# One branch at the end for all the seldom tiles of a sparse expert layer

## The chip, the cores and the metric

The kernel runs on one core of a Trainium2 chip. The metric is the device time of one launch in microseconds (us). Before the change it was 1567.93 us, the median of three runs (1567.35 to 1574.56).

## What is computed

The reference is one decoder layer for 2048 tokens of width 1024: a mixer (sliding-window attention, a gated linear recurrence and a forgetting attention, all from one input projection), then a hierarchical mixture of experts, then a final RMSNorm. The change lies in the mixture of experts. Each token picks one of 4 groups by its group logits, and in that group the best two of 4 experts:

```python
group_p, group_idx = lax.top_k(group_prob, 1)
top_p, top_local = lax.top_k(expert_prob, TOP_K)
weights = group_p * top_p / jnp.sum(top_p, axis=-1, keepdims=True)
for e in range(N_EXPERTS):
    hidden = jax.nn.silu(h @ w_gate[e]) * (h @ w_up[e])
    y = y + combine[..., e:e + 1] * (hidden @ w_down[e])
```

How many tokens go to an expert is known only once the router has run. The kernel computes an expert for its own tokens alone.

## The kernel before

**Lists.** The router (`router`, `place`) handles the 16 blocks of 128 tokens, a few at a time. It marks for each token its two experts and its group, counts marks per list with matmuls against a triangle and against ones, and scatters the token's number into 20 lists in HBM (`list_d`): one for each of the 16 experts (`NE`), and one for each of the 4 groups (`NL` = 20 in all). The list of the last group leaves out the tokens of the last expert. After the last block a matmul of ones with `cumM` gives the 20 lengths, and VectorE copies them as integers into `ci` (line 1072). At expert 0, line 1367 loads every length from `ci` into a register of each of the five engines, 20 loads on each.

**Experts.** `body(e)` computes two tiles of 128 tokens of expert e without a condition: a gather of token rows (`gather`), transposes (`x_T`), the gate and up products (`gates`), the down products (`down`), and a scatter with add into the residual stream in HBM (`add`). `chain(e, 2)` then covers a third tile and beyond: a branch on "length over 256" (line 1482) whose body computes a tile and holds the branch for the next one, 14 levels deep. A weight fetch for a later expert goes on SP's queue meanwhile.

**Final norm.** The tokens of a group can be normed and written when the group's four experts have been added. `fetch_done` and `fin_get` gather a finished group's tiles from the stream, `fin_rs` and `fin_scale` norm them (line 1539 is the scaling), and `fin_put` writes them to the output (line 1546). Six tiles (768 tokens) of each of the groups 0 to 2 are done so without a condition, two at a time within the bodies of later experts. `fin_chain(g, 6)` covers what a group has beyond 768 tokens: a branch (line 1554) around one tile and the next branch, 10 levels. For group 0 it stands after expert 6, for group 1 after expert 10.

**End.** `last_body` handles expert 15 and finishes that expert's tokens directly (`finish`, lines 1462 to 1469), with the two static tiles of the last group beside them. After the last write three blocks follow one another: `chain(15, 2)`, `fin_chain(2, 6)` and `fin_chain(3, 2)`.

**Order.** The program is written in order, and a planner with a simulated timeline places each instruction on its engine's queue. A conditional block is placed as one unit: nothing from outside goes between its instructions. `after(...)` and `behind(...)` add order edges by hand. Each engine runs the branch for itself when its own queue comes to it. An engine that jumps over a block afterwards brings up to date the semaphores that the block would have counted. In the records these are EVENT_SEMAPHORE and, for the DMAs that GpSimd (POOL) would have issued, INC_SWDGE_SEM; they stand under the line of the branch. Line 1624 is the end of the program: DRAIN, and semaphores between the engines.

## Time and profile before

| what | value |
|---|---|
| median of 3 runs | 1567.93 us |
| the profiled execution's own time | 1562.93 us |
| its span (first to last instruction) | 1561.1 us |
| mean granted clock of TensorE | 0.951 |
| instructions | 22860 |

The profiled execution was 5.00 us shorter than the median of the three runs, and 1.83 us of its time lie outside its span. PE is TensorE's matmul, PEld its weight load, DVE is VectorE, ACT is ScalarE, POOL is GpSimd and SP is SyncE; a name with a q after it (POOLq, DVEq) is that engine's sequencer, which runs branches, semaphores and register loads. Times in a row are us from the start of the span, unless marked ns.

### The profile page before, as it was taken

What the parts mean: (1) busy time and instruction counts of PE and PEld (TensorE: products, weight loads), DVE (VectorE), ACT (ScalarE), POOL (GpSimd) and SP (SyncE); (2) the same over time, 40 slices, a digit from 0 to 9 for tenths busy, and PEclk for the clock granted to TensorE, in tenths of its full rate; (3) what the DMA queues carried; (4) which work ended last, traced back from release to release, by engine and by line L of the source; (5) the groups of instructions that cost most, each with busy time, mean ns of one, the idle gap of its engine ahead of it and who ended that gap; (6) DMA issues with size and microseconds to landing.
All of it is one profiled execution on the core that took longest, in us unless ns stands there. A gap on an engine that the chain in (4) does not pass through costs nothing. (4 is left out here: it accounts for less than half of the span.)

```text
span 1561.1 us, 22860 instructions
## 1 busy us (share of the span) xinstructions
PE 1408.7 (90%) x6896; PEld 1131.8 (72%) x6896; DVE 1081.9 (69%) x2838; ACT 759.3 (49%) x1505; POOL 583.3 (37%) x662
## 2 busy tenths in 40 slices
PE   4799999989999899998899999995999998998981
PEld 4677789778898577776678877784777776776760
DVE  5767656745655998988856797785775665566664
ACT  5365234655655688987744232322553533343341
POOL 4210014102224554637704443433344434434452
PEclk9799999999999899999989999996999999999995
DMA  9527983156668856325164343325777868677954
GB/s 323 161 81 246 329 295 115 53 153 181 173 184 238 218 142 196 115 62 156 48 207 138 112 174 122 121 78 157 232 216 204 244 181 254 154 223 230 275 144 159
DMA packets 177087, 276.91 MB, mean 177 GB/s; under 512 B 31161, under 2 KB 120265, under 8 KB 176864
## 3 DMA queue, kind: packets, MB, share of 16 engines
q1 hardware_dynamic: 151184, 212.33, 43.4%
q0 software_dynamic: 25680, 62.09, 14.8%
q8 instruction: 81, 1.33, 0.4%
q14 instruction: 142, 1.16, 0.2%
HBM read 209.90 MB, written 89.03 MB: 191 GB/s over the span
## 5 line engine op out<-in xcount | busy, mean ns | idle before, releaser
L53 PE MATMUL sc<-R,R 128*128 128x512 f32 (+1 forms) x1352 | 324.7, 393 | 9.1 <-ACT R L131 5.4
L53 PEld LDWEIGHTS sc<-R,R 128*128 128x128 f32 x1352 | 249.4, 191 | 67.4 <-issue 7.8
L53 PE MATMUL sc<-R,yh 128*128 128x512 f32 x512 | 170.8, 412 | 10.0 <-DVE x L973 6.7
L855 POOL DMA_INDIRECT xg<-h_d,LT x55 | 63.4, 1153 | 171.3 <-PE sc L53 38.2
L53 PEld LDWEIGHTS sc<-R,yh 128*128 128x128 f32 x512 | 95.1, 193 | 32.6 <-DVE x L973 10.3
L132 DVE TENSOR_TENSOR ptlo<-tp,pthi 128x512 fp32r<-128x512 f32 (+3 forms) x162 | 98.1, 624 | 20.1 <-ACT pthi L131 19.6
L53 PE MATMUL sc<-R,hh 128*128 128x512 f32 x328 | 102.1, 413 | 3.8 <-DVE R L1462 3.1
L53 PE MATMUL sc<-R,fq 128*128 128x512 f32 (+3 forms) x320 | 96.8, 402 | 8.1 <-DVE fmx L287 4.5
L53 PE MATMUL sc<-R,yl 128*128 128x512 f32 x256 | 103.2, 404 | 0.0
L131 ACT ACTIVATE pthi<-tp 128x512 fp32r<-128x512 f32 (+3 forms) x162 | 85.0, 547 | 33.6 <-PE tp L306 15.1
L973 DVE SCALAR_TENSOR_TENSOR x<-sc,r,x 128x512 f32<-128x512 f32 x96 | 71.4, 746 | 41.4 <-PE sc L53 34.4
L53 PE MATMUL pv<-w,xh 128*128 128x512 f32 x256 | 84.3, 411 | 5.4 <-ACT xh L131 2.8
L53 PE MATMUL pv<-R,xh 128*128 128x512 f32 x256 | 85.5, 417 | 2.1 <-PEq L1482 0.9
L295 POOL TENSOR_SCALAR row<-row,frs 128x640 f32<-128x640 f32 (+11 forms) x48 | 71.7, 1495 | 38.5 <-DVE frs L294 32.1
L306 PEld LDWEIGHTS tp<-ident,row 128*128 128x128 f32 x504 | 62.8, 141 | 29.0 <-issue 14.0
L132 DVE TENSOR_TENSOR R<-R,R 128x512 fp32r<-128x512 f32 (+1 forms) x128 | 81.9, 698 | 0.3 <-ACT R L131 0.3
L306 PE MATMUL tp<-ident,row 128*128 128x128 f32 x504 | 78.5, 274 | 0.9 <-POOL row L295 0.9
L1128 POOL DMA_INDIRECT list_d<-vals,spots x48 | 50.6, 1054 | 70.9 <-DVE spots L1105 29.0
L131 ACT ACTIVATE R<-R 128x512 fp32r<-128x512 f32 (+1 forms) x130 | 73.3, 642 | 6.0 <-DMA R<-in_w_down 3.7
L53 PEld LDWEIGHTS sc<-R,hh 128*128 128x128 f32 x328 | 61.4, 196 | 17.0 <-DVE R L1462 3.8
L131 ACT ACTIVATE xh<-tp 128x512 fp32r<-128x512 f32 x82 | 45.4, 596 | 56.4 <-PE tp L1264 49.2
L293 ACT ACTIVATE row<-row,fmx 128x640 f32<-128x640 f32 (+11 forms) x48 | 68.0, 1416 | 8.5 <-DVE fmx L287 8.3
(414 smaller groups left out, 3439.2 us busy)
## 6 DMA issues: line engine op xcount, KB each, us to landing
x<-in_x SPq DMA_DIRECT2D x32, 512.0 KB
x<-in_w_mod SPq DMA_DIRECT2D x32, 512.0 KB
R<-in_w_gate SPq DMA_DIRECT2D x128, 128.0 KB
R<-in_w_up SPq DMA_DIRECT2D x128, 128.0 KB
R<-in_w_down SPq DMA_DIRECT2D x32, 512.0 KB
wraw<-in_w_inT SPq DMA_DIRECT2D x24, 512.0 KB
R<-kc_d SPq DMA_DIRECT2D x80, 128.0 KB
wm<-in_w_mod SPq DMA_DIRECT2D x32, 256.0 KB
```

The lines of the kernel that those rows point to most:

```text
L53: return PE.matmul(o, l, r, start=first, stop=last)
L131: return (ACT.activation(hi, src, AF.Copy), (lo_eng or V).tensor_tensor(lo, src, f32(hi), op=ALU.subtract))
L132: (lo_eng or V).tensor_tensor(lo, src, f32(hi), op=ALU.subtract))
L293: ACT.activation(row[:, 0:n], row[:, 0:n], AF.Exp, bias=prev, scale=-1.0, accum_out=rs)
L295: G.tensor_scalar(row[:, 0:n], row[:, 0:n], rs, 1.0, op0=ALU.mult, op1=ALU.mult)
L306: PE.transpose(p[:, r * 128:(r + 1) * 128], rows[r][:, j * 128:(j + 1) * 128], ident)
L855: return G.indirect_dma_start(out=dst, out_offset=None, in_=h2_d[:, :], in_offset=bass.IndirectOffsetOnAxis(ap=idx, axis=0), **(dict(bound ...
L973: V.scalar_tensor_tensor(x1[:, sl], p, r3s[t][:, g:g + 1], x1[:, sl], op0=ALU.mult, op1=ALU.add)
L1128: d = G.indirect_dma_start(out=list_d[:, :], out_offset=bass.IndirectOffsetOnAxis(ap=di[:, i, s:s + 1], axis=0), in_=vals[:, t0 + i, s, :] ...
```

## The change

The three branches at the end become one, on a new register, and the two branches in the middle go. The router computes the new number: `most` holds for each list how many tokens are covered without a condition (256 for expert 15 and group 3, 768 for groups 0 to 2, more than there can be for the other experts), a comparison with the lengths gives 20 zeros or ones, and their sum goes to `ci` as a 21st entry. The first 15 lengths and that entry are loaded into registers at expert 0, 16 loads for 20; the other five lengths are loaded inside the new block. Inside it stand the old three blocks and those of groups 0 and 1, whose lists are loaded again there.

```diff
+        most, seldom = cn.tile([1, NL], F32, name="most"), cn.tile([1, 1], F32, name="seldom")
+        V.memset(most, float(FAR))
+        V.memset(most[:, NE:NL - 1], 768.0)
+        for l in (NE - 1, NL - 1):
+            V.memset(most[:, l:l + 1], 256.0)
...
-                V.tensor_copy(ci, pc[0:1, 0:NL])
+                V.tensor_copy(ci[:, 0:NL], pc[0:1, 0:NL])
+                over = wk.tile([1, NL], F32, name="over", bufs=1)
+                V.tensor_tensor(over, pc[0:1, 0:NL], most, op=ALU.is_gt)
+                V.tensor_reduce(seldom, over, axis=AX.X, op=ALU.add)
+                V.tensor_copy(ci[:, NL:NL + 1], seldom)
...
-        ci = pers.tile([1, NL], I32, name="ci")
+        ci = pers.tile([1, NL + 1], I32, name="ci")
...
+        def length(l):
+            nreg[l] = nc.values_load_multi_w_load_instructions(ci[0:1, l:l + 1], ...)[1][0]
...
-                    for l in range(NL):
-                        nreg.append(nc.values_load_multi_w_load_instructions(ci[0:1, l:l + 1], ...)[1][0])
+                    for l in list(range(NE - 1)) + [NL]:
+                        length(l)
...
             with after([last]):
+                seldom_tiles(e)
+
+        def seldom_tiles(e):
+
+            with tc.If(nreg[NL] > 0):
+                for l in range(NE - 1, NL):
+                    length(l)
                 chain(e, 2)
+                fin_chain(NG - 1, 2, xg[1])
                 fin_chain(NG - 2, 6, xg[1])
-                fin_chain(NG - 1, 2, X5[nx[0] % 4])
+                for g in range(NG - 2):
+                    list_load(LG[g % 2], NE + g)
+                    fin_chain(g, 6, xg[1])
...
             if e < NE - 1:
                 chain(e, 2)
-            if e % 4 == 2 and 4 < e < NE - 2:
-                fin_chain(e // 4 - 1, 6, xg[1])
```

## Rows read from the trace of the kernel before

**Rows 1.** The page: busy us of each engine, share of the span, instructions.
```profile
PE 1408.7 (90%) x6896; PEld 1131.8 (72%) x6896; DVE 1081.9 (69%) x2838; ACT 759.3 (49%) x1505; POOL 583.3 (37%) x662
```

**Rows 2.** Stretches: start:end, us, busy us of PE, PEld, DVE, ACT, POOL, clock, DMA.
```profile
1500.00:1561.00 61.00, 25.65 (x95) 18.53 (x93) 32.68 (x98) 12.48 (x27) 22.65 (x20) 0.67 0.49 149
```

**Rows 3.** Order of time, POOL, last row: start, us, instruction, idle before it.
```profile
1546.15 0.97 POOL L1546 DMA_INDIRECT out_dram<-xg,LG  x1 [0.69 <-DVE xg L1539]
```

**Rows 4.** Line 1482 after 1540: ns min/median/max, first and last start.
```profile
L1482 POOLq EVENT_SEMAPHORE  x4: 17/43/43, 1546.4 to 1550.9; - x4
...
L1482 DVEq EVENT_SEMAPHORE  x1: 21/21/21, 1547.6 to 1547.6; - x1
L1482 POOLq INC_SWDGE_SEM  x1: 1088/1088/1088, 1551.0 to 1551.0; - x1
```

**Rows 5.** Line 1554 after 1540, the two later blocks of the end.
```profile
L1554 DVEq EVENT_SEMAPHORE  x2: 21/21/21, 1551.3 to 1554.8; - x2
L1554 POOLq INC_SWDGE_SEM  x2: 1073/1076/1079, 1552.8 to 1555.3; - x2
```

**Rows 6.** Line 1624, the end of the program.
```profile
L1624 POOLq DRAIN  x3: 50/114/3872, 1556.4 to 1560.9; - x3
```

**Rows 7.** Line 1554 on POOL over the whole span: branches at four places.
```profile
L1554 POOLq COMPARE_BRANCH  x4: 45/45/45, 1269.5 to 1553.9; - x4
```

**Rows 8.** Line 1554 on POOL from 1265 to 1280, the block of group 0.
```profile
L1554 POOLq EVENT_SEMAPHORE  x4: 17/43/43, 1269.9 to 1274.1; - x4
```

**Rows 9.** Order of time, POOL, around that block.
```profile
1269.74 1.80 POOL L1546 DMA_INDIRECT out_dram<-X,LG  x1 [14.13 <-DVE X L1539]
1275.95 1.33 POOL L1546 DMA_INDIRECT out_dram<-X,LG  x1 [4.41 <-DVE yo L1290]
```

**Rows 10.** Stretches of experts 6, 7, 9 and 11 (a branch of TensorE to the next).
```profile
1233.00:1249.40 16.40, 15.59 (x76) 12.32 (x77) 12.79 (x26) 11.80 (x24) 11.22 (x8) 1.00 0.87 219
1263.70:1282.70 19.00, 16.73 (x79) 12.74 (x80) 16.29 (x36) 11.91 (x24) 7.63 (x5) 1.00 0.48 149
1345.90:1362.10 16.20, 15.76 (x77) 12.75 (x78) 12.74 (x25) 9.83 (x20) 12.90 (x9) 1.00 0.82 217
1395.90:1414.70 18.80, 17.02 (x79) 12.93 (x80) 16.40 (x36) 11.92 (x24) 8.21 (x5) 1.00 0.46 144
```

**Rows 11.** TensorE's waits, 1200 to 1480: total, times, longest us.
```profile
PE tp L1272 <- DVEq L1482: 10.6, 6, 3.6
PE sc L53 <- DVE hl L132: 2.9, 2, 1.7
PE tp L1264 <- DMA xg<-h_d,LT: 2.8, 3, 1.5
```

**Rows 12.** Line 1482 on DVE from 1284 to 1294, expert 7's branch.
```profile
L1482 DVEq COMPARE_BRANCH  x1: 56/56/56, 1286.4 to 1286.4; - x1
L1482 DVEq EVENT_SEMAPHORE  x1: 21/21/21, 1292.0 to 1292.0; - x1
```

**Rows 13.** The same from 1476 to 1482, expert 13's branch.
```profile
L1482 DVEq COMPARE_BRANCH  x1: 56/56/56, 1477.4 to 1477.4; - x1
L1482 DVEq EVENT_SEMAPHORE  x1: 21/21/21, 1478.3 to 1478.3; - x1
```

**Rows 14.** Line 1367, the register loads.
```profile
L1367 SPq TENSOR_LOAD <-ci x20: 15/266/473, 1065.0 to 1089.2; - x20
...
L1367 ACTq TENSOR_LOAD <-ci x20: 275/280/478, 1082.8 to 1089.7; - x20
```

**Rows 15.** Order of time, DVE, at the end of the router.
```profile
1064.82 0.17 DVE L1072 CAST ci<-pv 1x20 int32<-1x20 f32 x1 [0.71 <-PE pv L53]
1066.12 0.16 DVE L1080 COPY rk<-pv 128x1 f32<-128x1 f32 x1 [1.13 <-PE pv L53]
```

**Rows 16.** Order of time, TensorE, from the router's end into expert 0.
```profile
1065.04 0.62 PE L53 MATMUL pv<-Ms,before 128*128 128x20 f32 x2 [0.26 <-DVE ci L1072]
...
1098.07 1.06 PE L1264 MATMUL tp<-ident,xg 128*128 128x128 f32 x8 [2.92 <-DMA xg<-h_d,LT]
```

## The prediction before the run

> **What bounds the kernel now.** The page's first part says TensorE: its matmuls are busy for 90% of the span, VectorE for 69% [rows 1]. That is an average, so the second view read is the table of stretches. In the last one TensorE works 25.65 us of 61.00 [rows 2]: the end of the program is bound by something else. The third view is the order of time at that end, and with it the records that the sequencers leave under the branch lines. POOL's last real work is the output write issued at 1546.15, 0.97 us long [rows 3], yet the span runs to 1561.1. So 14.0 us pass after it, and that is where the three branches stand. The fourth view is the list of TensorE's waits among the experts: 10.6 us in six waits end when VectorE gets past a branch of line 1482, 2.9 us with a VectorE result, 2.8 us with a gather [rows 11].

> **Whether the branches are taken.** Line 1554 has four sites in the program, and POOL shows four compares there [rows 7]; a taken one would show the next level's compare too. So no group has more than its static tiles. The count of the new register is a sum over the same comparisons, so it is zero and the new block is jumped over.

> **Part 1: three branches at the end become one.** A compare itself costs 45 ns [rows 7]. What costs is what follows it. On POOL the first block (line 1482) ends like this: its last EVENT_SEMAPHORE is at 1550.9, then INC_SWDGE_SEM from 1551.0 for 1.088 us, so to 1552.1 [rows 4]. The two blocks of line 1554 repeat branch, semaphores and INC_SWDGE_SEM; the second of these starts at 1555.3 and takes 1.07 us, to 1556.4 [rows 5]. POOL's DRAIN follows at 1556.4 and takes 3.872 us [rows 6], and everybody waits for it. The later two rounds are therefore 1556.4 - 1552.1 = 4.3 us, on the path. With one block POOL goes from 1552.1 straight to the DRAIN.

> The first round is not cheaper after the change. Its last semaphore at 1550.9 comes 3.8 us after the last write was issued (1546.15 + 0.97 = 1547.1), and I read it as a wait for that write to land; in the middle of the program the same four semaphores end at 1274.1, 2.6 us after a write issued by 1271.5 [rows 8, 9]. That wait also covers what the other engines need. VectorE gets past its first branch at 1547.6 and its later ones cost it until 1551.3 and 1554.8 [rows 4, 5], 3.7 and 3.5 us each; one jump instead of three leaves it ready before 1550.9. If POOL's own jump over the bigger block takes as long as VectorE's 3.7 us, it ends at 1549.6, still under the landing. Bounds: nothing gained, if the DRAIN ends when it does for another reason; up to 6.9 us, if two thirds of its 3.872 us (2.6 us) is the work of the two increments that go. I take 4.3, since the DRAIN starts in the row right where the last increment ends.

> [...]

> **Part 2: the two branches in the middle go.** At expert 6 POOL issues the first of two output writes at 1269.74, then meets the branch, whose semaphores run to 1274.1, so that the second write comes at 1275.95 instead of about 1271.9 [rows 8, 9]. POOL's queue behind it (gathers, adds) is 4 us late; expert 10 has the same, once. What does TensorE feel? Experts 7 and 11, behind those blocks, take 19.0 and 18.8 us from branch to branch, experts 6 and 9 take 16.4 and 16.2 [rows 10]. Three more matmuls at 0.21 us (15.59 by 76) are 0.6 of it. So 2.1 and 1.9 us are in excess. But not all of it is the branch: the two waits for a VectorE result, 2.9 us with the longest 1.7 [rows 11], stand behind the scaling of a finished pair of tiles, which stays (VectorE is busy for 16.3 us there, against 12.8 [rows 10]). That leaves 4.0 - 2.9 = 1.1 us. Of the three waits for a gather, 2.8 us with 1.5 the longest, I take one to come from POOL's late queue and count 1.1 us for it. Part 2 gives 2.2 us. Bounds: 0, if TensorE finds its data as late as before, and 4.0 + 1.1 = 5.1.

> **Part 3: four register loads fewer on each engine.** SP takes 24 us in all for its loads, with other DMAs between, ScalarE 20 loads from 1082.8 to 1090.0, 0.36 us each [rows 14]; four fewer are 1.4 us on ScalarE. Beside them TensorE waits 2.92 us, but for a gather that ends at 1098.07 [rows 16], which needs the lists and not ScalarE. So ScalarE's gain is covered. SP issues the list loads between its register loads; a pass there is three instructions, (1089.2 - 1065.0) / 19 = 1.3 us with all that lies between, and the loads' own 0.27 us bounds it from below. If all four went ahead of the lists, TensorE's 2.92 us would shrink by at most that. If instead the loads wait for the new entry of the same tile, they start some 0.5 us later. Bounds: 2.9 gained, 0.6 lost. I take 0.2 gained: what the planner puts ahead of the lists is set by when SP finds its weight buffers free.

> **Part 4: three small VectorE operations in the last step of the router.** The nearest rows are the copy to `ci`, 0.17 us, and the next copy, 0.16 us, which waits 1.13 us for TensorE [rows 15]. Reduce and cast fit in that wait. The comparison doesn't quite: it reads the bank that TensorE's next matmul waits for (0.26 us for the copy [rows 16]), so that matmul starts 0.1 to 0.2 us later, in a chain where nothing else runs. At worst all three stand there, 0.6 us; at best none, 0. I take 0.2 lost. The four memsets stand at the router's start, where TensorE has work of its own, and are single rows; cover gone, they cost a few tenths. The loads of the other five lengths, and the list loads on SP, lie inside the block and are jumped.

> **The sum.** -4.3 - 2.2 - 0.2 + 0.2 = -6.5 us. The profiled execution took 1562.93 us (span 1561.1 and 1.83 around it), so its like after the change takes 1556.4. The median of the runs stood 5.00 us above it, and I keep that: 1567.93 - 6.5 = 1561.4, or 0.41% less. With the terms' likely play its own range is 1558.5 to 1565. 0.5%, about what a measurement of this kernel can tell from no change, is 7.8 us: faster begins below 1560.1, slower above 1575.8.

> **Rivals.**
> - *The middle gives more.* Experts 7 and 11 fall to the length of 6 and 9 (5.1 us with the gather), and the end gives 4.3 to 6.9: 1555.9 to 1558.5, say 1557. For it: DMA share in these stretches is 0.48 and 0.46 against 0.87 and 0.82, POOL issues 5 against 8 and 9 [rows 10], so more than TensorE is held up. Against it: VectorE's scaling stays.
> - *Slower: VectorE's fetch behind the expert branches falls worse.* At expert 13 it goes on 0.9 us after the compare [rows 13], at expert 7 only after 5.6 us, of which TensorE idles 3.6 [rows 11, 12]. Which of the two a branch meets should depend on where its target lies in VectorE's stream, and taking two blocks out of that stream moves every target from expert 7 to 14. Each branch that turns from quick to slow costs up to 3.6 us. Two use up the gain (1561.4 + 7.2 = 1568.6, from where it is slower than before), three give 1572, four 1575.8. Against it: the slow ones can turn quick as well, and with 10.6 us in six waits, 3.6 the longest, several are slow already.
> - *The end is held by something else* (the DRAIN ends when it ended, or a branch really costs no more than its compare), and the middle gives nothing: about 1567.8, two compares of 45 ns less. Against it are the DRAIN's start and VectorE's 3.5 us behind a jump [rows 5, 6].
> - *The block is taken*: then it costs five loads and at least one further round of tile, gather and write. Rows 7 exclude it for these inputs.

> **How the numbers follow.** The forecast gets 0.48, the better middle 0.25, the worse fetch 0.17, the held end 0.08, the taken block 0.02. Faster by over 0.5%: the better middle and a third of the forecast's own range, 0.40. Slower by over 0.5%: the worse fetch with four branches or more and half of the taken block, 0.06. Within: 0.54. The range reaches from 1554 (both upper bounds of the parts 1 and 2, with no more) to 1571 (between two and three branches worse).

> **What would show it.** Part 1: one INC_SWDGE_SEM after the last output write, the DRAIN about 1 us after that write's landing, and 9.7 us instead of 14.0 from the last write to the end. If the DRAIN grows by what the rounds lose, part 1 is wrong. Part 2: POOL's two output writes of expert 6 next to one another, and stretches of experts 7 and 11 nearer 18 us. Part 3: 16 loads in each queue, TensorE's wait before expert 0's second transposes still near 2.9 us. Part 4: the wait behind the copy to `ci` near 0.4 us. The waits on VectorE's branch tell the slower rival: 10.6 us now; above 17 it has come true.

## The result, and the profile after

The changed kernel took 1551.72 us (median of 7 runs, 1550.02 to 1557.07), the kernel before beside it 1567.35 us (7 runs). Its time is 0.9929 of that of before, 95% interval [0.9900, 0.9958]: 11.1 us less (6.6 to 15.7 by the interval). A second set (experiment 11) gave 0.9949 [0.9926, 0.9971], 8.0 us less (4.5 to 11.6). On the 1567.93 us of the prediction these are 1556.8 and 1559.9 us; the forecast was 1561.4. Single runs of one kernel lie up to 1.5% apart, so what follows goes by ratios of many runs and by stretches of the profile. The profiled execution took 1554.04 us (span 1552.2), for 1562.93 before.

**The end.** The changed kernel's last row of POOL in order of time, then its line of the new branch after 1538 (ns min/median/max, first and last start), then the end of the program. They answer to [rows 3 to 6].

```profile
1542.08 0.96 POOL L1569 DMA_INDIRECT out_dram<-xg,LG  x1 [0.69 <-DVE xg L1562]
```
```profile
L1461 POOLq EVENT_SEMAPHORE  x5: 17/43/43, 1545.0 to 1545.9; - x5
...
L1461 DVEq EVENT_SEMAPHORE  x2: 21/21/21, 1543.4 to 1543.5; - x2
L1461 DVEq COMPARE_BRANCH  x1: 56/56/56, 1540.5 to 1540.5; - x1
L1461 POOLq COMPARE_BRANCH  x1: 53/53/53, 1541.8 to 1541.8; - x1
L1461 POOLq INC_SWDGE_SEM  x1: 1110/1110/1110, 1546.0 to 1546.0; - x1
```
```profile
L1645 POOLq DRAIN  x3: 46/109/3872, 1547.1 to 1551.6; - x3
```

One round stands where three stood. The last write ends at 1542.08 + 0.96 = 1543.0, the last semaphore comes at 1545.9, the increment ends at 1547.1, and the DRAIN, as long as before to the nanosecond, follows at once. That last semaphore is a wait for the write to land, that is, for its data to have arrived: in the trace the landing is counted at 1545.87, and in the kernel before, where the semaphore came at 1550.89, at 1550.86. From the last write to the end it is 9.1 us, for 14.0 before. POOL's own jump (1541.8 to 1545.0) is over before the last semaphore.

**The middle.** POOL's two output writes of expert 6 in order of time, which answer to [rows 9]:

```profile
1269.13 1.81 POOL L1569 DMA_INDIRECT out_dram<-X,LG  x1 [1.21 <-DVE X L1562]
1271.24 1.00 POOL L1569 DMA_INDIRECT out_dram<-X,LG  x1 [0.30 <-issue]
```

The stretches of experts 6, 7, 9 and 11 (columns as in [rows 10]), and TensorE's waits from 1200 to 1480, which answer to [rows 11]:

```profile
1232.50:1248.70 16.20, 15.57 (x76) 12.30 (x76) 12.73 (x26) 11.79 (x24) 11.09 (x8) 1.00 0.88 227
1263.00:1281.90 18.90, 16.56 (x79) 12.80 (x80) 16.33 (x36) 11.79 (x24) 15.08 (x7) 1.00 0.78 203
1342.30:1358.40 16.10, 15.68 (x77) 12.71 (x78) 12.66 (x25) 9.83 (x20) 11.04 (x8) 1.00 0.82 217
1392.10:1409.40 17.30, 16.59 (x81) 13.42 (x82) 15.02 (x29) 11.91 (x24) 12.84 (x8) 1.00 0.88 212
```
```profile
PE tp L1277 <- DMA xg<-h_d,LT: 6.5, 1, 6.5
PE tp L1285 <- DVEq L1505: 4.6, 5, 3.7
PE sc L53 <- DVE xl L132: 2.8, 2, 2.0
...
PE sc L53 <- DVE hl L132: 2.2, 2, 1.7
```

The writes now follow one another, but expert 7 is as long as before (18.90 for 19.00 us). The gain of this part lies in expert 8, from 63.2 to 60.4 us between TensorE's branches (62.9 in experiment 1, which keeps the two blocks, 60.0 in experiment 2, which leaves them out alone). Its waits there, first before (1282.7 to 1345.9), then after (1281.9 to 1342.3):

```profile
PE tp L1272 <- DVEq L1482: 3.6, 1, 3.6
PE tp L1264 <- DMA xg<-h_d,LT: 2.8, 3, 1.5
```
```profile
PE tp L1285 <- DVEq L1505: 3.7, 1, 3.7
PE sc L53 <- DVE xl L132: 0.8, 1, 0.8
```

All three gather waits of [rows 11], 2.8 us, stood in expert 8, and all are gone. The waits on VectorE's branch fell from 10.6 to 4.6 us: those of 2.9 and 3.3 us at the starts of experts 12 and 13 are gone. A wait of 6.5 us for a gather in expert 14 is new.

**Router and loads.** VectorE and then TensorE at the router's end, TensorE before expert 0's second transposes, and the loads; they answer to [rows 14 to 16].

```profile
1061.93 0.17 DVE L1078 CAST ci<-pv 1x20 int32<-1x20 f32 x1 [0.71 <-PE pv L53]
1062.03 0.15 DVE L1080 TENSOR_TENSOR over<-pv,most 1x20 f32<-1x20 f32 x1
...
1063.38 0.16 DVE L1090 COPY rk<-pv 128x1 f32<-128x1 f32 x1 [0.82 <-PE pv L53]
```
```profile
1062.33 0.58 PE L53 MATMUL pv<-Ms,before 128*128 128x20 f32 x2 [0.44 <-DVE over L1080]
```
```profile
1095.25 1.59 PE L1277 MATMUL tp<-ident,xg 128*128 128x128 f32 x8 [3.94 <-DMA xg<-h_d,LT]
```
```profile
L1263 SPq TENSOR_LOAD <-ci x16: 260/266/475, 1062.1 to 1083.2; - x16
...
L1263 ACTq TENSOR_LOAD <-ci x16: 274/283/478, 1078.3 to 1083.9; - x16
```

TensorE waits 0.44 us behind the comparison, for 0.26 behind the copy. There are 16 loads, and the wait for expert 0's gather is 3.94 us, for 2.92.

### The profile page after: what moved, and what is told of

It is laid out like the page before. It is cut to its first block, busy times and chain, and to the rows that moved or that the text cites. A ratio compares the mean times of both kernels' runs of the same rounds, so it can differ in the third digit from the quotient of the medians.

```text
span 1552.2 us, 22799 instructions
## 1 busy us (share of the span) xinstructions
PE 1405.7 (91%) x6896; PEld 1130.2 (73%) x6896; DVE 1084.0 (70%) x2845; ACT 759.2 (49%) x1505; POOL 590.4 (38%) x662
## 3 DMA queue, kind: packets, MB, share of 16 engines
q14 instruction: 132, 1.08, 0.2%
```

## The experiments

All ratios are to the kernel before, run on the same chip in the same set. The stretches are from each kernel's profiled execution, in us: from TensorE's last branch of expert 6 to that of expert 11, from there to that of expert 14, and from the end of POOL's last write to the end of the span (tail). The last column counts the packets of one queue of instructions, spoken of at the end.

```
kernel                            ratio   95% interval        7-11  12-14   tail    q14
before (blocks in the middle: 2)  1                          166.1   69.7   14.0    142
1  middle kept, one at the end    0.9981  [0.9951, 1.0012]   165.2   72.4    9.6    137
8  six rounds at the end          1.0051  [1.0029, 1.0072]   168.7   74.7   20.0    150
changed                           0.9929  [0.9900, 0.9958]   163.0   68.0    9.1    132
11 changed, again                 0.9949  [0.9926, 0.9971]   163.0   67.6    9.7    132
2  middle alone                   0.9958  [0.9928, 0.9989]   160.7   67.7   13.6    137
3  the same, padded               0.9960  [0.9929, 0.9991]   161.8   69.7   13.4    138
4  changed, padded                0.9920  [0.9895, 0.9945]   161.7   71.0    9.6    134
7  changed, no block at the end   0.9908  [0.9881, 0.9935]   160.6   69.0    4.7    124
9  changed, block before writes   0.9914  [0.9881, 0.9946]   160.8   68.2    5.7    132
5  eight blocks in the middle     1.0165  [1.0121, 1.0209]   178.8   84.6   13.4    156
6  eight, without transfers       1.0087  [1.0053, 1.0120]   175.5   73.2   13.4    152
10 eight, without the norm        1.0011  [0.9989, 1.0033]   162.6   75.2   13.2    146
12 changed, short expert blocks   0.9811  [0.9771, 0.9850]   155.2   57.7    8.8     87
```

**1 and 2: the end and the middle apart.** In 1 the two middle blocks stand again in the changed kernel (their two lengths are loaded at expert 0 again, 18 loads); 2 is the kernel before without them.

```diff
 # 1, on the changed kernel
                 chain(e, 2)
+            if e % 4 == 2 and 4 < e < NE - 2:
+                fin_chain(e // 4 - 1, 6, xg[1])
 # 2, on the kernel before
-            if e % 4 == 2 and 4 < e < NE - 2:
-                fin_chain(e // 4 - 1, 6, xg[1])
```

Expected of 1: 

> The change without its middle part: the blocks of groups 0 and 1 stand again after experts 6 and 10, the end has the one branch (over three lists), 18 loads. Theory A (placement: the gain among the experts comes from where VectorE's jumps land, the gain at the end from the two rounds that go): only the end is left, 4.5 to 5.5 us below the kernel before (ratio 0.9965 to 0.9971); last write to end 9 to 10 us; VectorE's stalls behind experts 11 to 13 as before (TensorE idles 2.9 and 3.3 us at experts 12 and 13). Theory B (load: POOL's queue is freed of two blocks): the same total, and the same stalls. Theory C (all of the 11 us is the end and the router): 10 to 11 us below, ratio 0.993.

Expected of 2: 

> The kernel before without the two blocks in the middle and nothing else (what groups 0 and 1 have beyond 768 tokens is left out, which is nothing here). Theories A and B: 3 to 7 us below the kernel before (ratio 0.9955 to 0.998), the three rounds at the end stay (14 us from last write to end). VectorE's jumps land 3 to 5 instructions from where they land in the changed kernel, so by A experts 12 and 13 lose their idle time there too. Theory C: no difference, 1.000.

Measured: 3.0 us less (1565.79 x 0.0019) for the end, 6.6 us less for the middle. The interval of the first reaches from 7.7 us less to 1.9 more, so the ratio alone does not show the end's gain; the tail does, 9.6 us for 13.2 to 14.0 in the six kernels with three rounds. The two parts add up, within the intervals, to what the whole change gives. Theory C, by which the end is everything, falls. Experiment 1's profile still shows TensorE idle for 2.3 and 3.2 us at experts 12 and 13, as both other theories said.

**3 and 4: where VectorE's jumps land.** 3 is the kernel of 2, and 4 the changed kernel, each with VectorE instructions added in a level that never runs; nothing that runs is different, and each engine's order of work is the same.

```diff
-        MID_K = 7
-        yos = [None]
+        MID_K, PAD, nopad = 7, {6: 150, 10: 149}, yp.tile([1, 1], F32, name='nopad', bufs=1)
+        yos, pad = [None], lambda e, t: [V.memset(nopad, 0.0) for i in range(PAD.get(e, 0) if t == NT - 1 else 0)]
...
-                    chain(e, t + 1)
+                    pad(e, t) ; chain(e, t + 1)
```

In 4 the number is `{6: 64}`.

Expected of 3: 

> The same as the one before, with 150 and 149 tiny VectorE instructions in the deepest level, which never runs, of the blocks of experts 6 and 10: VectorE's program is as long there as in the kernel before, and nothing that runs is different. Theory A: the stalls behind experts 11 to 13 are back (2 to 4 us each at experts 12 and 13), and most of the gain of the unpadded one is gone: ratio to before 0.998 to 1.000. Theory B: the same as unpadded, within 0.1%.

Expected of 4: 

> The changed kernel with 64 tiny VectorE instructions in the deepest level, which never runs, of the block of expert 6: every later VectorE jump starts and lands 64 instructions further on. Theory A: other branches among experts 7 to 14 are quick and slow than in the changed kernel, and the time moves by 2 to 8 us in either direction. Theory B: the same as the changed kernel within 0.1%, 11 us below the kernel before.

Measured: the ratios 0.9960 and 0.9920, those of the kernels without padding (0.9958; 0.9929 and 0.9949) within their intervals. But the jumps do change. VectorE behind expert 11's last branch and at expert 13's, first in 2, then in 3 (a compare, and the semaphore where VectorE goes on; the second compare at expert 11, of 47 ns, stands right behind that semaphore):

```profile
L1482 DVEq COMPARE_BRANCH  x2: 47/52/56, 1427.7 to 1428.6; - x2
L1482 DVEq EVENT_SEMAPHORE  x1: 21/21/21, 1428.5 to 1428.5; - x1
...
L1482 DVEq COMPARE_BRANCH  x1: 56/56/56, 1464.7 to 1464.7; - x1
L1482 DVEq EVENT_SEMAPHORE  x1: 21/21/21, 1472.5 to 1472.5; - x1
```
```profile
L1482 DVEq COMPARE_BRANCH  x2: 47/52/56, 1423.7 to 1426.6; - x2
L1482 DVEq EVENT_SEMAPHORE  x1: 21/21/21, 1426.5 to 1426.5; - x1
...
L1482 DVEq COMPARE_BRANCH  x1: 56/56/56, 1465.5 to 1465.5; - x1
L1482 DVEq EVENT_SEMAPHORE  x1: 21/21/21, 1466.4 to 1466.4; - x1
```

Unpadded it is 0.8 us at expert 11 and 7.8 at expert 13; padded, with the targets where they lie in the kernel before, 2.8 and 0.9. So placement decides which jump is quick, which the slower rival needed. That the total followed from it, as theory A had it, is not shown. For 3 that theory wanted 0.998 to 1.000, which the interval only just reaches. What one branch gains another loses, or a wait for a gather takes it (5.2 us in expert 14 in 3, 3.6 in 2).

**5, 6 and 10: the price of a block in the middle.** Eight blocks after experts 6 to 13 for two: as they are, without the transfers, and without the norm.

```diff
-            if e % 4 == 2 and 4 < e < NE - 2:
-                fin_chain(e // 4 - 1, 6, xg[1])
+            if 6 <= e <= 13:
+                fin_chain(0 if e < 10 else 1, 6, xg[1])
 # 6: fin_get and fin_put left out for groups 0 and 1;  10: fin_calc left out for them
```

Expected of 5: 

> The kernel before with eight blocks in the middle for two: one after each of experts 6 to 13 (group 0 up to expert 9, group 1 from then on), all jumped over. Without the two blocks the kernel before lost 6.5 us (0.7 to 11) by ratio, and 3.9 us in the stretch from expert 7 to 11 by the profiles. Theory P (POOL, when it jumps a block with transfers in it, first waits for its own transfers to land and then counts them up, so that the gathers behind it are late) and theory V (VectorE fetches instructions behind each jump, 0.8 to 5.6 us): six more blocks cost 2 to 3.2 us each, 12 to 20 us, ratio 1.008 to 1.013. Theory N (the two blocks cost next to nothing, what was measured came from the order of other work): 1.000 within 0.002.

Expected of 6: 

> The same eight blocks without the gathers and writes in them (left out: what a taken block would fetch and write); ScalarE's and VectorE's instructions stay, every engine branches as before, and POOL has no transfer to count up. Theory P: the price of the blocks goes: 3 to 7 us below the kernel before, ratio 0.9955 to 0.998, like the kernel without middle blocks. Theory V: the price stays, ratio 1.006 to 1.013. Half of each: 1.002.

Expected of 10: 

> The eight middle blocks with their gathers and writes, without the norm in them (left out: ScalarE's and VectorE's instructions in these blocks, so that VectorE and ScalarE jump over branches alone); the planner then puts some of the blocks a few instructions earlier. With all, eight blocks cost 25.9 us more than two; without transfers 13.6 us more than two; two cost 6.5 us against none. Theory S (the two parts add: POOL's share is what is missing without transfers, 32.4 - 20.1 = 12.3 us for eight): 12 us above no block, 6 us above the kernel before, ratio 1.002 to 1.006. Theory P (POOL's landing wait is the price, and the rest of the run without transfers was order): 26 us above the kernel before, ratio 1.013 to 1.018. Theory V (VectorE's jump is the price): as without middle blocks, 0.995 to 0.998.

Measured: +25.9, +13.6 and +1.7 us against the kernel before. Against the kernel with no middle block (experiment 2, 6.6 us below before) eight blocks cost 32.5, 20.2 and 8.3 us: 4.1, 2.5 and 1.0 us each. (Experiment 2's own interval, 1.7 to 11.3 us, makes each of these prices uncertain by some 0.6 us and more.) Theory N falls, and neither P nor V is the whole: with VectorE's and ScalarE's instructions alone a block costs 2.5 us, with the transfers alone 1.0, and together (3.5) they nearly make the price. The two overlap, since in both every engine still branches: behind its own branch (PEq) TensorE waits 5.9, 6.1 and 8.7 us in 5, 6 and 10, for 2.7 before.

The wait for a landing, of theory P, stands in neither part. In 10 the blocks stand a few instructions earlier, and no transfer still under way holds POOL at them: in all eight its last semaphore comes within 0.7 us of the compare. In 5 it comes after 4.6, 0.4, 6.4, 0.7, 4.6, 0.7, 11.4 and 0.7 us. POOL at expert 12's block (line 1554), in 5 (compare at 1483.6), then in 10 (compare at 1457.9):

```profile
L1554 POOLq EVENT_SEMAPHORE  x4: 17/43/10827, 1484.0 to 1495.1; - x4
```
```profile
L1554 POOLq EVENT_SEMAPHORE  x4: 17/43/43, 1458.3 to 1458.5; - x4
```

For that wait only the 0.6 us are left that 3.5 lacks of 4.1, and the intervals do not resolve them. So what it costs by itself is open; leaving out the transfers also takes POOL's instructions out of the block. The waits of TensorE from 1200 to 1480 show which part is which, in 5 and in 6:

```profile
PE tp L1272 <- DVEq L1482: 10.5, 7, 3.5
PE tp L1264 <- DMA xg<-h_d,LT: 8.4, 3, 4.5
```
```profile
PE sc L53 <- DVE hl L132: 9.7, 6, 2.9
PE pv L53 <- PEq L1482: 6.1, 8, 2.7
PE tp L1272 <- DVEq L1482: 5.4, 6, 3.4
```

With transfers TensorE waits 8.4 us for gathers; without, 9.7 us for results that VectorE brings late.

**7 and 8: the end.** 7 leaves the last block out, 8 adds three rounds to the kernel before.

```diff
 # 7, on the changed kernel
-            with after([last]):
-                seldom_tiles(e)
 # 8, on the kernel before
                 fin_chain(NG - 1, 2, X5[nx[0] % 4])
+                for i in range(3):
+                    fin_chain(NG - 2, 6, xg[1])
```

Expected of 7: 

> The changed kernel without the block at the end (the seldom tiles are left out, which are none here). In the changed kernel 9.1 to 9.6 us pass from the last write to the end. If the one round left costs its INC_SWDGE_SEM, 1.1 us go (8.0 to 8.5 us, ratio to before 0.9915 to 0.9925). If the end needs the same landing and the same counting without a block, nothing goes (9.1 to 9.6, ratio 0.992 to 0.9935). If the jump itself stands on the path, 3 us go.

Expected of 8: 

> The kernel before with six blocks at the end for three (that of group 2 three times more), all jumped over. Theory of the prediction (each round costs what the later two cost, 2.15 us): 20.0 to 20.5 us from the last write to the end for 13.4 to 14.0, 6.5 us more in all, ratio 1.004. Rival (VectorE's jumps, 3.5 us each, set the pace): 24 us, 10.5 us more, ratio 1.007. If a branch costs no more than its compare: 14 us and 1.000.

Measured in 8: 20.0 us from the last write to the end. Against the mean of the kernels with three rounds (13.5), three more cost 6.4 us, 2.1 each, as the prediction had it; by ratio 8.0 us [4.5, 11.3]. The compare-only theory falls, and so does the rival's 24 us. In 7 it is 4.7 us, less than all three expectations. (Its ratio, 0.9908, lies below the changed kernel's two, with overlapping intervals.) POOL's last write and the DRAIN there:

```profile
1555.42 0.96 POOL L1567 DMA_INDIRECT out_dram<-xg,LG  x1 [0.69 <-DVE xg L1560]
```
```profile
L1643 POOLq DRAIN  x3: 46/115/5072, 1555.2 to 1560.8; - x3
```

Without a block the DRAIN begins before the last write and ends at 1560.3, 3.9 us after it. So the one round that the change leaves still stands on the path with 4.4 to 5 us. In the changed kernel the wait for the landing (2.9 us), the increment (1.1) and the DRAIN (3.9) follow one another; without a block the DRAIN runs while the last write is under way.

**9: the block ahead of the last writes.** From that reading: POOL jumps the block before the last four writes.

```diff
             for t in range(2):
-                    finish(e, t, xs[t])
+                    finish(e, t, xs[t], False)
...
-                    fin_calc(fs[t:t + 1])
-                last = fin_put(*fs[t])
-            with after([last]):
+                    last = fin_calc(fs[t:t + 1])
+            with after(last):
                 seldom_tiles(e)
+            for t in range(2):
+                behind(token_put(e, t, xs[t]), 1)
+                behind(fin_put(*fs[t]), 1)
...
```

Expected: 

> The changed kernel with its one block moved ahead of the last four output writes: POOL jumps it while VectorE still works out what these writes carry, the other engines as before behind their last work (group 1's list goes into group 0's buffer there, since the last write still reads the other one). Without any block 4.7 us pass from the last write to the end, with it 9.1 to 9.6. Theory of the end (the landing, the counting and the jump stand on the path only because they come behind the last write): 4.7 to 5.2 us from the last write to the end, the last write no later, ratio to the kernel before 0.9895 to 0.992, some 4 us below the changed kernel. Rival (POOL's jump of the big block, 3 us, its waits and the counting delay the four writes): last write 2 to 4 us later, tail 4.7 us, 0 to 2 us below the changed kernel. Second rival (the wait for landings is for what other engines count, VectorE's last work among it, and so the block ends as late as before): tail 4.7, last write after VectorE's end by 5 us, nothing gained.

POOL in order of time, then the new branch's line:

```profile
1529.43 0.97 POOL L1578 DMA_INDIRECT out_dram<-X,LG  x1 [0.31 <-issue]
1538.43 0.96 POOL L1502 DMA_INDIRECT out_dram<-R,LT  x1 [8.03 <-DVE rq_u L106]
...
1542.35 0.96 POOL L1578 DMA_INDIRECT out_dram<-xg,LG  x1 [0.30 <-issue]
```
```profile
L1464 POOLq EVENT_SEMAPHORE  x5: 17/43/9538, 1526.6 to 1536.4; - x5
...
L1464 POOLq INC_SWDGE_SEM  x1: 1030/1030/1030, 1536.5 to 1536.5; - x1
```

The first rival comes nearest: one semaphore holds POOL for 9.5 us, until 1536.3, when the write issued at 1529.43 lands (counted at 1536.26). So the last four writes come late, the last one 50.4 us after TensorE's branch of expert 14, for 48.1 and 48.2 in the changed kernel, and the tail is 5.7 us, where the rival had 4.7. From TensorE's branch of expert 14 to the end it is 57.1 us, for 58.1 and 58.9 in the two profiles of the changed kernel: 1 to 2 us gained. The ratio 0.9914 beside 0.9949 of the same set doesn't tell the two apart.

**11: the changed kernel again.**

Expected: 

> The changed kernel itself, once more, for a closer ratio and a second profile. If the 11.1 us hold: ratio 0.992 to 0.9945. The prediction's sum, 6.5 us, would be 0.9958. Which of VectorE's branches are quick should be the same as in the first profile (experts 3, 4, 10, 11 and 13), if where the target lies decides; single stalls of ScalarE or a wait of 6.5 us for a gather in expert 14 may come or go.

Measured: 0.9949. The same branches are quick (experts 3, 4, 10, 11, 13), the stretches agree within 0.5 us from expert 4 on, and the wait in expert 14 is there again with 6.3 us. It is no accident of one execution.

**12: short blocks.** The middle block's price hung on what is jumped (2.5 us each in 6, 1.0 in 10), and the experts' own blocks are jumped as well: each expert's chain ends with one jump, some after a taken level or more.

```diff
-            if t < NT:
+            if t < 6:
                 lt = LT[e % NLT]
                 with tc.If(nreg[e] > t * 128, label=f"more{e}_{t}"):
-                    if t < NT - 1:
+                    if t < 5:
...
-                    if t + 1 < NT:
+                    if t < 5:
```

Expected: 

> The changed kernel with the experts' conditional blocks cut from fourteen levels to four (left out: an expert's seventh tile and beyond, which no expert has here). What runs is the same; VectorE's jump from the branch to its target is 40 to 50 instructions long for 140 to 183. In the changed kernel most of VectorE's jumps take 2.4 to 6.6 us and bring an instruction packet of 8 KB, five take 0.8 us and bring none, and TensorE waits 3.7 us behind one of them in expert 8. Theory V (the price of a jumped block is mostly this fetch): most of VectorE's jumps take 0.8 us, TensorE's waits on VectorE's branch go, 4 to 12 us below the changed kernel, ratio to the kernel before 0.985 to 0.991. Rival P (POOL's waits for its landings set the pace of the experts, and what VectorE gains is given back in waits for a gather): VectorE's jumps as by V, the ratio 0.991 to 0.995, as the changed kernel. If the jumps stay slow, the fetch doesn't hang on the length, and the time is the changed kernel's.

Measured: 29.7 us less than before, 19 to 22 below the changed kernel and more than theory V asked. Its waits of TensorE from 1200 to 1480:

```profile
PE sc L53 <- DVE xl L132: 3.4, 2, 2.1
...
PE tp L1285 <- DVEq L1505: 0.4, 1, 0.4
```

The wait on VectorE's branch is down to 0.4 us, and no wait for a gather is left, where rival P wanted one in its place. For POOL's jumps are quick too, but for those of experts 7 and 14, where 5.8 and 3.8 us pass to the first semaphore. POOL at expert 10, first the changed kernel, then 12:

```profile
L1505 POOLq EVENT_SEMAPHORE  x4: 17/43/43, 1389.3 to 1389.5; - x4
L1505 POOLq COMPARE_BRANCH  x1: 53/53/53, 1382.8 to 1382.8; - x1
```
```profile
L1505 POOLq EVENT_SEMAPHORE  x2: 43/43/43, 1381.9 to 1382.0; - x2
L1505 POOLq COMPARE_BRANCH  x1: 53/53/53, 1381.7 to 1381.7; - x1
```

6.5 us from POOL's compare to its first semaphore became 0.2. How the gain is shared between VectorE's jumps and POOL's, this run doesn't tell. An expert with over 768 tokens would need its last tiles in the block at the end; that form was not run.

## Why the prediction was right, and where it was off

- **Part 1, the end (-4.3).** Right in mechanism and size: 13.2 to 14.0 us with three rounds, 9.1 to 9.7 with one (8.8 in experiment 12), 4.0 us between the means. The DRAIN didn't grow (3.872 us in both), which puts the upper bound of 6.9 out; the tails, and experiment 8's six rounds, put out the lower one, nothing.
- **Part 2, the middle (-2.2).** The mechanism was right in part and the size too small: 6.6 us by ratio, whose interval [1.7, 11.3] still holds the forecast; 8.6 by the six blocks that experiment 5 adds (25.9 / 6 = 4.3 each); and by the stretches of experts 7 to 14 in single profiles 7.4 (before less experiment 2) and 6.6 (experiment 1 less the changed kernel). All four lie over the upper bound of 5.1. Two readings failed. "Stretches of experts 7 and 11 nearer 18 us" looked in the wrong place: expert 7 kept its length, and the first stretch of expert 11 fell by 1.5 us, which its third tile lost again (1409.4 to 1421.5, 12.1 us for 10.6). POOL's lateness was felt one expert on, in expert 8, where all 2.8 us of the gather wait stood; I counted 1.1 of it. And the price of jumping VectorE's and ScalarE's instructions, some 2.5 us per block in experiment 6, was in no term, though VectorE's 3.7 and 3.5 us at the end showed it [rows 4, 5].
- **Part 3, the loads (-0.2), and part 4, the router (+0.2).** Nothing that a run resolves. The wait for expert 0's gather was 3.94 us where near 2.9 was forecast, and 16 loads didn't shorten it; the wait behind the comparison was 0.44 us, as forecast.
- **The sum.** -6.5 us forecast; -8.0 and -11.1 measured. The two parts by themselves make -9.6 (experiments 1 and 2). The first set has the size of the rival "the middle gives more" (1556.8 us for its 1557), the second that of the forecast's own range; the reason is neither one's length of experts 7 and 11. That the total lies as near the forecast as it does is in part luck: in experts 12 to 14 two waits on VectorE's branch (2.9 and 3.3 us) went and a gather wait of 6.5 us came, and the sum had neither. A slip in the range: both upper bounds of parts 1 and 2 give 1555.9, not 1554.
- **The slower rival.** Its mechanism is real: padding alone turned jumps from 0.8 to 2.8 us (expert 11 in 3) and from 7.8 to 0.9 (expert 13). It did not come true: TensorE's wait on VectorE's branch went to 4.6 us, far from 17. Its price per branch was too simple: several branches turned in experiments 3 and 4, and the time stayed.
- **The held end and the taken block.** Both out: 4 us went, and the block's body left no record.

That experts 12 to 14 are some 3.5 us shorter without the middle blocks (72.3 us in the mean with two, 68.7 without) is seen in the profiles. How much of it is VectorE's placement and how much POOL's queue stays open, and so does the cause of the new gather wait in expert 14: experiment 1, which keeps the middle blocks, has one of 5.2 us too.

## What to carry to other kernels

A conditional block that is never taken still had a price here: 4.1 us each in the middle (experiment 5) and 2.1 at the end (experiment 8), for a compare of 45 ns. So count the instructions that each engine must pass over (2.5 us a block in experiment 6) and the transfers whose counts it must make up (1.1 us for the increment at the end), not the compare. Merge blocks that are seldom taken and take them out of the loop (8.0 and 11.1 us less here), and above all keep the code that is jumped short (another 19 to 22 us less in experiment 12). Look for a queue's lateness not only in the step behind the delay but in the next one that has no slack: here the 2.8 us stood in expert 8, not in 7.

## What the runs showed of the hardware

```profile
q14 instruction: 1, 0.01, 1.0%
```

The fourteen profiles have 217 such jumps of VectorE over what is left of an expert's chain. 71 take 0.2 to 1.3 us, and in 65 of them no packet of q14 starts; 146 take 2.0 to 7.8 us, and in 141 of them at least one does. (Packets of q14 start at other times too, in the changed kernel 117 of 132, so one within a jump need not be VectorE's; and long jumps hold other work as well, as expert 7's of 5.6 us in the kernel before holds 2.48 us of scalings.) The five slow ones without a packet are all expert 12's, of 2.5 us, and are no slow jumps: in the changed kernel VectorE's two scalings, queued ahead of that branch (compare at 1446.2), end at 1448.6, and the semaphore follows at 1448.7.

```profile
1446.14 2.48 DVE L1562 SCALAR_TENSOR_TENSOR X<-X,rs,R 128x1024 f32<-128x1024 f32 x2
```

Over the whole execution of the changed kernel the same queue carried (packets, MB, share):

```profile
q14 instruction: 132, 1.08, 0.2%
```

Over all fourteen profiles (last column of the table) fewer packets go with less time, from 87 at a ratio of 0.9811 to 156 at 1.0165, nearly in order; that by itself does not tell which brings which. The fetch of which the slower rival and the expectations speak shows in these traces only as such packets. Counted in the program, the jumps of the changed kernel pass over 142 to 183 VectorE instructions, and were quick or slow by where they landed (experiments 3 and 4). In experiment 12 they pass over 12 to 53, and all among the experts were quick (0.8 us at expert 8's last branch, for 2.7 in the changed kernel), but for the scalings at expert 12. A packet holds some 8 KB (1.08 MB / 132). Why one place of landing comes with a packet and another with none, these runs don't tell.
